# A two-layer hybrid block: each stream of the recurrent part gets its own build-time priority

## The chip, the cores and the metric

The program runs on one core of one Trainium2 chip, in one launch. The metric is the device time in microseconds (us) of that launch. Before the change the median of three runs is 3154.19 us (3151.38 to 3157.79); one further execution was taken with the hardware profiler.

## The reference, cut to what matters

Two layers work on 256 latent and 256 context tokens of width 1024. Each layer is a gated feed-forward part, a mixer with three branches (banded attention, an RWKV-7 recurrence, an S5 recurrence) that a gated sum merges, and a second feed-forward part. The change lies in the recurrent part of the mixer, the RWKV-7 branch:

```python
def rwkv7_scan(state0, r, decay, k, v, kk, kka, reverse):
    def step(state, inp):
        r_t, w_t, k_t, v_t, kk_t, b_t = inp
        state = (state * w_t[:, :, None, :]
                 - jnp.einsum('bhvk,bhk->bhv', state, kk_t)[..., None] * b_t[:, :, None, :]
                 + v_t[..., None] * k_t[:, :, None, :])
        return state, jnp.einsum('bhvk,bhk->bhv', state, r_t)
...
    s_f, ocf = rwkv7_scan(zero, rc, dfc, kc, vc, kkc, bc, reverse=False)
    s_b, ocb = rwkv7_scan(zero, rc, dbc, kc, vc, kkc, bc, reverse=True)
    _, olf = rwkv7_scan(s_f, rl, dfl, kl, vl, kkl, bl, reverse=False)
    _, olb = rwkv7_scan(s_b, rl, dbl, kl, vl, kkl, bl, reverse=True)
```

Eight heads of 64 channels are scanned forwards and backwards, first over the context, then over the latent tokens. Everything is in float32.

## The kernel before, in words

The kernel does not step token by token. It takes the heads in four pairs (p = 0 to 3) and the tokens in chunks of 64. For each pair, class Rwkv writes its work as generators:

- `operands()`: first `common()` (the low-rank inputs shared by all pairs), then `prep(p)`: it fetches or makes the pair's columns (`mixed`, `column`: a product with `w_in` whose weights go through `split`, lines 131 to 138), makes decay, normalised key and the chunk operands AR and BK. It stands still at marked places (`yield`), among them once after each of the two scan directions (d = 0, d = 1; lines 614 to 642).
- `fronts()`: `front(p)`: Gram products of the chunks (line 680, masked by L683), then the inverse of small triangular systems, the "solve": DMAs that gather 16x16 blocks, a chain of VectorE products and sums that each need the one before (L708, L709), DMAs that bring the result back (L727, L735).
- `turns()`: transposed operands. `backs()`: the rest of the inverse by TensorE products (L794) and VectorE (L803 to L819).
- `chains()`: the recurrence itself, eight chunk steps per pair, each TensorE, ScalarE (Y, L850), TensorE, both (Z, L863, L865), TensorE, VectorE (S, L878, L882).
- `ends()`: `finish(p)`: group norm, bonus and gate.

`conduct` (line 979) writes these generators into one program: it keeps a clock of its own that the generators' yields advance, always continues the first stream in its list that is due, and where none is due it continues a filler: dense products that have nothing to do with the recurrence (the gates and the remaining columns first, then the projections of the other branches). Layer 1 has all 15 of its recurrent columns made ahead and stored, layer 0 only 6; the other 9 are made inside `operands()`.

Two things set the order on the engines. TensorE's instructions stay in the order in which `conduct` wrote them (`manual_schedule` for PE). For VectorE (DVE), ScalarE (ACT), GpSimd (POOL) and the DMA queue of SyncE (SP), a planner orders the instructions when the program is built: it steps through a planned time, and an engine that is free takes, among the instructions whose inputs are ready in that plan, the one with the best priority. The priority is the place in the written program; `high_priority(offset=n)` counts an instruction as written n places earlier. Each engine then runs its list in that fixed order on the chip, whatever the real times. Before the change every one of the six streams has the same offset, HIGH = 300, and the filler has none:

```python
        with nullcontext() if s is filler else k.tc.high_priority(offset=HIGH):
            v = next(s.g, StopIteration)
```

The weights of the filler and of `column` pass through `split`: a DMA on SP (wr, L135), a rounded copy on ACT (wh, L136) and the remainder on DVE or, every second time in this part, on POOL (wl, L137); `mm3` multiplies with them in three products (L153 and L154 with wh, L155 with wl). Three buffers each hold wr, wh and wl, and two more each in layer 1's recurrent part.

Of the kernel before, what the change touches and what calls it, by code (L numbers as in the profile page):

```python
# [25 lines left out]
HIGH = 300  # L26
# [6 lines left out]
class Ctx:  # L33
    def __init__(self, ctx, tc):
        self.tc, self.nc = tc, tc.nc
        nc = self.nc
        self.cp = ctx.enter_context(tc.tile_pool(name="consts", bufs=1))
        self.wp = self.pool(ctx, "w")
        self.up = ctx.enter_context(tc.tile_pool(name="u", bufs=16))
        self.tp = ctx.enter_context(tc.tile_pool(name="tiny", bufs=2))  # L40
        self.dp = ctx.enter_context(tc.tile_pool(name="dram", bufs=1, space=DRAM))
        self.uid = 0
        self.aside = False
        self.mm = None
# [454 lines left out]
class Rwkv:  # L499
# [431 lines left out]
    def streams(self):  # L931

        pr = [{} for _ in range(4)]

        def chains():
            for p in range(4):
                yield f"prep{p}"
                yield from self.chain(pr[p])

        def turns():  # L940
            for p in range(4):
                yield f"prep{p}"
                for st in range(2):
                    yield from self.turn(pr[p], st)

        def backs():
            for p in range(4):
                yield f"front{p}"
                for st in range(2):
                    yield from self.back(pr[p], st)  # L950

        def ends():
            for p in range(4):
                yield f"chain{p}.1"
                yield from self.finish(pr[p])

        def operands():
            yield from self.common()
            for p in range(4):
                yield from self.prep(p, pr[p])  # L960

        def fronts():
            for p in range(4):
                yield f"prep{p}"
                yield from self.front(pr[p])

        return [Stream(g) for g in (fronts(), chains(), turns(), backs(), operands(), ends())]


class Stream:  # L970
# [1 line left out]

    def __init__(self, g):
        self.g, self.at, self.need = g, 0.0, None


def conduct(k, done, streams, filler, now, until):


    filler, dve = Stream(filler), now
    filler.at = now
    todo = streams + [filler]
    while filler in todo or until not in done:
        ready = [s for s in todo if s.need is None or s.need in done]
        s = next((s for s in ready if s.at <= now), None)
        if s is None:
            now = min(s.at for s in ready)
            continue  # L990
        with nullcontext() if s is filler else k.tc.high_priority(offset=HIGH):
            v = next(s.g, StopIteration)
        s.need = None
        if v is StopIteration:
            todo.remove(s)
        elif isinstance(v, str):
            s.need = v
        else:
            v = v if isinstance(v, tuple) else (1.0 if v is None else v, 0.3, None)
            now += v[0]  # L1000
            if len(v) == 3:
                dve = max(dve, now) + v[1]
            s.at = now if v[-1] is None else (now if len(v) == 2 else dve) + v[-1]
    return now, [s for s in todo if s is not filler]
# [596 lines left out]
def mixer(k, first, l, a, u, src, mods, mrows, acst, tab, ctx_out, spill):  # L1601
# [49 lines left out]
    with ExitStack() as es:  # L1651
        k.more_weights(es, f"mix{l}", None)
        with ExitStack() as e2:
            k.sp, k.qp = k.pool(e2, f"s5{l}"), k.pool(e2, f"att{l}")
            k.more_weights(e2, f"mixa{l}", (4, 4, 4))
            columns()
            k.sums.close()
            k.psum(e2, f"mixa{l}", 2, 2)
            rw = Rwkv(k, l, a, u, w_in, pf, ctx_out)
            dense = seq(rw.columns(), gates())  # L1660
            weave(k, local(), dense, W0[l], False)
            while rw.left:
                next(dense)
        k.more_weights(None, None, None)
        with ExitStack() as e2:
            e2.enter_context(tc.manual_schedule(engines={mybir.EngineType.PE}))
            k.psum(e2, f"mixr{l}", 2)
            k.sp, k.ep = k.pool(e2, f"rwl{l}"), k.pool(e2, f"rwe{l}")
            k.aside = True
            if not ctx_out:  # L1670
                k.more_weights(e2, f"mixr{l}", (2, 2, 2))
            streams = rw.streams()
            with ExitStack() as e3:
                k.qp = k.pool(e3, f"prep{l}")
                now, streams = conduct(k, rw.done, streams, dense, 0.0, "prep3")
            with ExitStack() as e3:
                k.qp = k.pool(e3, f"proj{l}")
                conduct(k, rw.done, streams, project(), now, "finish3")
            k.aside = False
# [179 lines left out]
```

## Time and profile before

| | before |
|---|---|
| median of 3 runs | 3154.19 us |
| profiled execution, its own time | 3158.24 us |
| its span, first to last instruction | 3156.4 us |
| mean granted TensorE clock | 0.931 |
| TensorE busy | 2774.0 us (88%) |
| VectorE, ScalarE, GpSimd busy | 1598.4, 1075.0, 747.4 us |

Instructions of the recurrent parts run from about 792 to 1270 us (layer 0) and from about 2490 to 2892 us (layer 1). Engines are named PE (TensorE), PEld (its weight loads), DVE, ACT, POOL and SP. "L803" is line 803 of the kernel; `X<-pt` says which tile is written from which.

### The profile page before, as it was taken

How to read it: one execution, taken by the hardware profiler on the slowest of the kernel's cores; microseconds unless marked ns; L12 is line 12 of the kernel's file. 1: busy time of each engine (PE TensorE's matmuls, PEld its weight loads, DVE VectorE, ACT ScalarE, POOL GpSimd, SP SyncE). 2: the span in 40 equal slices, each digit the busy share in tenths (PEclk: the TensorE clock that was granted, in tenths of full speed). 3: DMA queues.
4: the chain of work that ended last, by engine and by line, in shares of the span. 5: the costliest groups of instructions: out<-in, count | busy, mean ns of one | idle time of the engine just before them, and what ended most of it. 6: DMA issues, size and time to landing. Idle time of an engine off the chain costs nothing. (4 is left out here: it accounts for less than half of the span.)

```text
span 3156.4 us, 52345 instructions
## 1 busy us (share of the span) xinstructions
PE 2774.0 (88%) x19886; PEld 2184.1 (69%) x19886; DVE 1598.4 (51%) x3363; ACT 1075.0 (34%) x2132; POOL 747.4 (24%) x940
## 2 busy tenths in 40 slices
PE   4999999899887789889999989999988876688798
PEld 2666787658665566666678876778766775577697
DVE  4655235394355554542322577623559156654555
ACT  3222224244343322242232343322433352323453
POOL 1333004010232213430100335311311242113311
PEclk8999999999998889899999999999999797788899
DMA  7786544924442343568843354453482544154564
GB/s 225 210 245 200 155 142 138 236 66 121 117 109 48 71 97 96 185 196 269 269 122 94 110 137 126 119 158 121 120 216 75 140 129 109 34 122 139 167 186 152
DMA packets 656824, 455.22 MB, mean 144 GB/s; under 512 B 158982, under 2 KB 580980, under 8 KB 648380
## 3 DMA queue, kind: packets, MB, share of 16 engines
q1 hardware_dynamic: 604096, 415.30, 46.2%
q10 hardware_dynamic: 52476, 36.58, 4.2%
q8 instruction: 156, 2.56, 0.3%
q14 instruction: 96, 0.79, 0.1%
HBM read 391.26 MB, written 64.18 MB: 144 GB/s over the span
## 5 line engine op out<-in xcount | busy, mean ns | idle before, releaser
L153 PE MATMUL acc<-u,wh 128*128 128x512 f32 (+1 forms) x2544 | 935.2, 368 | 72.2 <-ACT wh L136 31.8
L155 PE MATMUL acc<-u,wl 128*128 128x512 f32 (+1 forms) x2544 | 917.6, 361 | 48.7 <-DVE wl L137 34.4
L154 PE MATMUL acc<-u,wh 128*128 128x512 f32 (+1 forms) x2544 | 917.1, 361 | 13.1 <-POOL u L289 9.9
L137 DVE TENSOR_TENSOR wl<-wr,wh 128x512 fp32r<-128x512 f32 x720 | 536.6, 754 | 758.1 <-ACT wh L136 746.1
L136 ACT CAST wh<-wr 128x512 fp32r<-128x512 f32 x844 | 513.2, 619 | 1055.9 <-PE acc L154 540.9
L153 PEld LDWEIGHTS acc<-u,wh 128*128 128x128 f32 x2544 | 499.5, 196 | 183.0 <-ACT wh L136 41.9
L155 PEld LDWEIGHTS acc<-u,wl 128*128 128x128 f32 x2544 | 499.7, 196 | 136.4 <-DVE wl L137 42.2
L154 PEld LDWEIGHTS acc<-u,wh 128*128 128x128 f32 x2544 | 500.4, 197 | 90.2 <-POOL u L289 17.9
L137 POOL TENSOR_TENSOR wl<-wr,wh 128x512 fp32r<-128x512 f32 x124 | 171.9, 1392 | 590.7 <-ACT wh L136 565.8
L365 POOL TENSOR_TENSOR hl<-sg,hh 128x512 fp32r<-128x512 f32 (+1 forms) x88 | 107.7, 1224 | 639.4 <-ACT hh L364 597.9
L398 PE MATMUL acc<-wl,hh 128*128 128x512 f32 x616 | 242.1, 393 | 0.0
L399 PE MATMUL acc<-wh,hl 128*128 128x512 f32 x616 | 242.1, 394 | 0.0
L397 PE MATMUL acc<-wh,hh 128*128 128x512 f32 x616 | 242.0, 393 | 0.0
L362 DVE TENSOR_TENSOR sg<-sg,acc 128x512 f32<-128x512 f32 (+1 forms) x88 | 54.6, 620 | 185.0 <-PE acc L155 184.8
L211 PE MATMUL pt<-wa,cond 128*32 128x512 f32 x576 | 101.5, 669 | 40.4 <-DMA wa<-in_w_ada_dram 40.4
L398 PEld LDWEIGHTS acc<-wl,hh 128*128 128x128 f32 x616 | 115.6, 188 | 25.7
L397 PEld LDWEIGHTS acc<-wh,hh 128*128 128x128 f32 x616 | 115.7, 188 | 25.5
L399 PEld LDWEIGHTS acc<-wh,hl 128*128 128x128 f32 x616 | 115.6, 188 | 25.4
L289 POOL TENSOR_TENSOR u<-v,u 128x256 fp32r<-128x256 f32 x88 | 71.4, 828 | 89.0 <-DVE v L288 86.6
L364 ACT CAST hh<-sg 128x512 fp32r<-128x512 f32 (+1 forms) x88 | 49.8, 566 | 105.0 <-DVE sg L362 104.8
L794 PE MATMUL pt<-X,X 64*64 64x64 f32 x1536 | 60.6, 242 | 26.6 <-DVE X L803 22.1
L794 PEld LDWEIGHTS pt<-X,X 64*64 64x64 f32 x1536 | 56.5, 156 | 32.2 <-issue 23.8
(345 smaller groups left out, 3633.2 us busy)
## 6 DMA issues: line engine op xcount, KB each, us to landing
wr<-in_ffn_w_in_dram SPq DMA_DIRECT2D x372, 256.0 KB
wa<-in_w_ada_dram SPq DMA_DIRECT2D x64, 1024.0 KB
wr<-in_w_in_dram SPq DMA_DIRECT2D x216, 256.0 KB
wr<-in_ffn_w_out_dram SPq DMA_DIRECT2D x176, 256.0 KB
s5r<-s5tab SPq DMA_DIRECT2D x24, 512.0 KB
wr<-in_branch_proj_dram SPq DMA_DIRECT2D x48, 256.0 KB
s5tab<-s5wo SPq DMA_DIRECT2D x64, 128.0 KB
s5tab<-s5wi SPq DMA_DIRECT2D x64, 128.0 KB
```

What stands on the lines that cost most here:

```text
L136: nc.scalar.copy(hi, raw)
L137: (nc.gpsimd if aside else nc.vector).tensor_tensor(lo, raw, hi.bitcast(F32), ALU.subtract)
L153: nc.tensor.matmul(ps, wh, xh, start=first, stop=False)
L154: nc.tensor.matmul(ps, wh, xl, start=False, stop=False)
L155: i = nc.tensor.matmul(ps, wl, xh, start=False, stop=last)
L211: nc.tensor.matmul(ps[32 * ci:32 * ci + 32, :], cond[:, kk, :], w[:, 512 * ci:512 * ci + 512], start=(kk == 0), stop=(kk == 7))
L289: nc.gpsimd.tensor_tensor(lo, v, hi.bitcast(F32), ALU.subtract)
L365: nc.gpsimd.tensor_tensor(h_lo[:, :ntok], sg[:, :ntok], h_hi.bitcast(F32)[:, :ntok], ALU.subtract)
L397: nc.tensor.matmul(ps, hh[f][:, tk], ws[0], start=n == 1, stop=False)
L398: nc.tensor.matmul(ps, hh[f][:, tk], ws[1], start=False, stop=False)
L399: nc.tensor.matmul(ps, hl[f][:, tk], ws[0], start=False, stop=n == nf)
L794: nc.tensor.matmul(ps[rows, j * C:(j + 1) * C], lhs(j, h, rows), rhs[rows, j * C:(j + 1) * C], start=True, stop=True)
```

## The change

Each stream carries its own offset in place of the common 300: fronts and chains 900, backs 600, turns and ends 300, operands 0. An offset of 0 is that of the filler. The program text that `conduct` writes, and with it the order on TensorE, depends on the yields alone and stays; no instruction is added or removed by the edit.

```diff
-        return [Stream(g) for g in (fronts(), chains(), turns(), backs(), operands(), ends())]
+        return [Stream(g, HIGH * x) for g, x in ((fronts(), 3), (chains(), 3), (turns(), 1), (backs(), 2), (operands(), 0), (ends(), 1))]
...
-    def __init__(self, g):
-        self.g, self.at, self.need = g, 0.0, None
+    def __init__(self, g, ahead=0):
+        self.g, self.ahead, self.at, self.need = g, ahead, 0.0, None
...
-        with nullcontext() if s is filler else k.tc.high_priority(offset=HIGH):
+        with k.tc.high_priority(offset=s.ahead) if s.ahead else nullcontext():
             v = next(s.g, StopIteration)
```

## Rows read from the trace of the kernel before

**Rows 1.** Stretches: length, busy us (instructions) of each engine, PE clock, DMA share.
```profile
945.00:1120.00 175.00, 132.62 (x1938) 106.97 (x1934) 101.26 (x208) 54.55 (x132) 39.02 (x48) 0.85 0.27 60
...
2490.00:2640.00 150.00, 102.93 (x847) 95.12 (x847) 71.27 (x104) 69.51 (x131) 54.14 (x49) 0.85 0.57 149
2640.00:2760.00 120.00, 84.52 (x1572) 72.62 (x1570) 75.38 (x173) 39.82 (x104) 20.52 (x24) 0.78 0.22 45
```

**Rows 2.** TensorE's waits, 792 to 1270 us: us in total, times, longest.
```profile
PE pt L794 <- DVE X L803: 19.7, 3, 9.2
PE pt L857 <- ACT Y L850: 18.6, 11, 6.5
PE acc L155 <- DVE wl L137: 11.0, 2, 9.3
...
PE acc L155 <- POOL wl L137: 4.8, 2, 4.0
```

**Rows 3.** TensorE's waits, 910 to 927 us.
```profile
PE acc L153 <- ACT wh L136: 3.5, 1, 3.5
```

**Rows 4.** TensorE's waits, 2490 to 2892 us.
```profile
PE pt L794 <- DMA X<-sysr: 18.8, 3, 15.8
PE acc L155 <- DVE wl L137: 17.0, 3, 12.3
PE pt L857 <- ACT Y L850: 14.4, 15, 5.5
PE acc L153 <- ACT wh L136: 14.0, 2, 12.6
```

**Rows 5.** Timeline of DVE from 830 us: start, us, engine, line, operation, tiles, count.
```profile
830.41 1.39 DVE L635 TENSOR_TENSOR AR<-dc,kk 128x252 f32<-128x252 f32 x1
...
834.03 0.42 DVE L642 TENSOR_TENSOR BK<-dc,z 64x256 f32<-64x256 f32 x1
834.48 1.29 DVE L137 TENSOR_TENSOR wl<-wr,wh 128x512 fp32r<-128x512 f32 x2
```

**Rows 6.** Timeline of ACT from 911 us.
```profile
911.08 0.29 ACT L634 COPY AR<-kk 128x4 f32<-128x4 f32 x2
...
913.71 1.66 ACT L136 CAST wh<-wr 128x512 fp32r<-128x512 f32 x3
```

**Rows 7.** Timeline of POOL from 914 us.
```profile
914.98 2.94 POOL L642 TENSOR_TENSOR BK<-dc,z 64x256 f32<-64x256 f32 x4
917.88 3.12 POOL L137 TENSOR_TENSOR wl<-wr,wh 128x512 fp32r<-128x512 f32 x2
```

**Rows 8.** Timeline of SP, DMA issues from 2496 us.
```profile
2496.08 0.43 SPq L565 DMA_DIRECT2D lw<-in_rwkv_w_dram  x1
...
2498.68 0.98 SPq L135 DMA_DIRECT2D wr<-in_w_in_dram  x2
```

**Rows 9.** Timeline of DVE from 2608 us.
```profile
2608.01 0.94 DVE L635 TENSOR_TENSOR AR<-dc,kk 128x252 f32<-128x252 f32 x1
2608.88 0.67 DVE L709 TENSOR_REDUCE sysT<-X 128x64 f32<-128x512 f32 x1
...
2614.81 0.42 DVE L642 TENSOR_TENSOR BK<-dc,z 64x256 f32<-64x256 f32 x1
2615.26 1.89 DVE L137 TENSOR_TENSOR wl<-wr,wh 128x512 fp32r<-128x512 f32 x3
```

**Rows 10.** Timeline of ACT from 990 us.
```profile
990.03 1.28 ACT L615 ACT_TABLE_LOAD   x1
...
996.32 0.25 ACT L850 COPY Y<-pt 128x128 f32<-128x128 f32 x1
```

**Rows 11.** Line 635 from 785 to 1130 us: duration ns min/median/max.
```profile
L635 DVE TENSOR_TENSOR AR<-dc,kk x16: 414/422/1401, 821.3 to 1100.3; 128x252 f32<-128x252 f32 x16
```

**Rows 12.** Timeline of TensorE: the Gram products of pair 2, layer 0.
```profile
1035.40 0.83 PE L680 MATMUL pt<-AR,BK 64*128 64x128 f32 x10
```

**Rows 13.** Timeline of DVE: the last operands of pair 2, layer 0.
```profile
1022.51 0.76 DVE L642 TENSOR_TENSOR BK<-dc,z 64x256 f32<-64x256 f32 x2
```

**Rows 14.** Groups on DVE by form, 2713 to 2719 us: busy us, mean ns.
```profile
L683 DVE TENSOR_TENSOR G<-pt,cst 128x512 f32<-128x512 f32 x4 | 2.5, 681 | 0.0
L683 DVE TENSOR_TENSOR G<-pt,cst 128x256 f32<-128x256 f32 x4 | 1.5, 418 | 0.1
```

## The prediction

> **What bounds the kernel now.** I read the stretches first. TensorE is the busiest engine, but not in the recurrent parts: from 945 to 1120 us it works 132.6 of 175 us, and 102.9 of 150 and 84.5 of 120 us in two stretches of layer 1, at a granted clock of 0.85, 0.85 and 0.78 of full speed, means of time at its two levels of 1.2 and 2.4 GHz [rows 1]. There it is held by others, so the second view is the list of its waits. They fall into two kinds. The first are waits of the recurrence itself: 19.7 us on X of `back`, 18.6 on Y of `chain` in layer 0 [rows 2], 14.4 on Y and 18.8 on the solve's DMA in layer 1 [rows 4]. The second are waits of dense products on a split of their weights: 11.0 on VectorE and 4.8 on GpSimd in layer 0 [rows 2], 3.5 on ScalarE [rows 3], 17.0 on VectorE and 14.0 on ScalarE in layer 1 [rows 4]. The third view, the timeline of the engine that ended each long wait, shows the same in nearly all: a run of `prep` instructions of the next pair just ahead of the one that TensorE needs.
>
> **What the change can move.** It changes offsets, so it moves an instruction only where two are ready together in the plan and the new difference of offsets turns their order. Two cases have to be kept apart.
>
> Streams against each other (900, 600, 300 in place of 300 for all): the written order already decided between them, and `conduct` writes in TensorE's order. The second half of a pair's operands is written behind the normalisation's products (L190), and the chain's step of that moment stands ahead of these. So Y of 996.32 us had the better place already, and still ran behind 6.3 us of `prep` on ScalarE (from 990.03, where a table load of 1.28 us begins) [rows 10]: the plan did not have it ready when the chip did. A higher offset does not cure that. The recurrence's waits could fall by anything from nothing to all 52.7 us of the three largest VectorE and ScalarE rows (19.7 + 18.6 + 14.4); I take 3 us, near the lower end, for the few short operations (a finish, an early `prep` part) that were written earlier and ready.
>
> Operands against the filler (0 against 0, before 300 against 0): here the order does turn. Until now every `prep` instruction went ahead of a filler split written up to 300 places earlier. Now the written order decides, and since `conduct` gives the filler its turn between the two directions of the operands (the yield between them states 4.6 us of VectorE time), a column begun there has its splits ahead of the second direction.
>
> - Layer 0, wait of 9.3 us [rows 2]: the split at 834.48 had eight `prep` instructions of the second direction ahead of it, from 830.41 on [rows 5]. It gains 834.48 - 830.41 = 4.1; the first direction stays ahead. Bounds 0 and 9.3.
> - Layer 0, 910 to 927 us: 3.5 on ScalarE [rows 3], 4.0 on GpSimd and 11.0 - 9.3 = 1.7 on VectorE [rows 2]. ScalarE's cast at 913.71 stood behind `prep` from 911.08: 2.6. GpSimd's split stood behind four L642, 2.9 [rows 6, 7]. With the 1.7 that is 7.2; bounds 0 and 9.2.
> - Layer 1, 12.6 us at its start [rows 4]: on SP the weight load at 2498.68 was issued behind the operand loads that begin at 2496.08 [rows 8]; `common` stays ahead, the pair's loads go behind: 2.6. Bounds 0 and 12.6, because the weights' landing is most of it.
> - Layer 1, the other two VectorE waits: 17.0 - 12.3 = 4.7; I take 4.0, the size of the second direction in layer 0. Bounds 0 and 4.7.
> - Layer 1, 12.3 us [rows 4]: the split at 2615.26 had `prep` ahead from 2608.01, with one solve reduction of 0.67 that stays ahead [rows 9]: 7.25 - 0.67 = 6.6. Bounds 0 and 12.3.
>
> Together 3 + 4.1 + 7.2 + 2.6 + 4.0 + 6.6 = 27.5 us.
>
> **What it gives back.** The moved splits now run beside GpSimd's half of the operands. L635 takes 414 ns alone and up to 1401 ns in these runs [rows 11]; I charge the difference, 1.0 us, at five places: 5 us; bounds 0 and 7. The operands come later by the splits put ahead of them (0.7 us each); their reader, the Gram products, had room where I looked: the last operand of pair 2 began at 1022.51 and the products at 1035.40, 12.1 us after its end [rows 12, 13]. So no charge there; without that room each 0.7 would show. Last, part of each removed wait comes back at the next one: three weight buffers let a split run only a column or so ahead, and TensorE arrives sooner at the next. I take a third, 9.2 us, between nothing and all of it. The nine columns that layer 0 makes inside `operands()` lose their 300 places too; they then come in TensorE's own order with the filler's, which is worth nothing either way in the sum. The sum is 27.5 - 5 - 9.2 = 13.3 us.
>
> The Trainium skill has a rule that speaks against this part ("SBUF — State Buffer", Who interferes with whom): a VectorE instruction with two SBUF inputs and a GpSimd instruction that reads SBUF exclude each other, and whichever is issued second waits the other out in full. The spread of L635 agrees [rows 11]. By it a moved split could wait out a whole GpSimd operand, and the GpSimd one a moved split: my estimate from the page's rule is twice the 5 us, and the sum would be 8.3 us instead of 13.3.
>
> **From the profiled execution to the median.** The rows come from an execution of 3158.2 us (span 3156.4, 1.8 around it). 3158.2 - 13.3 = 3144.9. That execution was 4.0 us above the median of 3154.2, so the median to expect is 3141.
>
> **The rivals.**
>
> 1. *The recurrence gains too.* If the planner did hold the chain's and the solve's instructions back in favour of the operands, X, Y and the solve win: half of 19.7 + 18.6 + 14.4 and half of the longest solve wait of 15.8, 34 us more: 3107. For it: the runs of `prep` stand right ahead of these too [rows 10]. Against it: equal offsets and the written order already favoured them.
> 2. *Next to nothing changes.* The splits were not ready in the plan either when the operands began, or the next wait takes all of the gain. Then within 6 us of before: 3153. For it: the Y case shows that plan and chip differ by microseconds. Against it: TensorE waited at L155, with the first two products of the same weights behind it, so the cast that the split needs had long been done.
> 3. *Slower: the operands starve.* With the lowest rank, each handoff of a pair's normalisation (square, root, spread, two products that TensorE waits for) can find a mask block of `front` ahead on VectorE: eight L683 are 2.5 + 1.5 = 4.0 us [rows 14]. Three pairs per layer run beside another pair, each with two handoffs: 12 x 4.0 = 48 us at most. It decides from 27.5 - 14.2 = 13.3 us, some four of the twelve; with six of them, 24 us, the result is 3154.2 - 13.3 + 24 = 3165. For it: TensorE's order is fixed, so a late product stops all behind it. Against it: the Gram products of the pair before stand ahead of these handoffs in TensorE's order, so their masks are mostly done by then.
>
> **How the numbers follow.** About 0.2%, 6.3 us, is what a measurement can tell from no change. Chances: the forecast 0.50 (own range 3126 to 3150), rival 1 0.12, rival 2 0.20, rival 3 0.18. Faster: 0.12 and nearly all of 0.50, 0.60 in all; same 0.22 (rival 2 and the upper edge of the forecast); slower 0.18. The range reaches down to half of rival 1's extra gain, which leaves 0.08 below, and up to 3161, which takes in rival 2 and the first part of rival 3 and leaves about 0.12 above: 3118 to 3161. The five splits' upper bounds (9.3 + 9.2 + 12.6 + 4.7 + 12.3 = 48.1) lie below its lower end and count to the part left out; all lower bounds with the charge of 7 fall at 3161.
>
> **What the changed profile would show.** TensorE's waits on wl L137 by VectorE fall from 11.0 to about 7 in layer 0 and from 17.0 to about 6 in layer 1; that on GpSimd's from 4.8 to about 1; the 12.6 at layer 1's start to about 10, with the weight load ahead of z and v on SP. X on L803 and Y on L850 stay above 30 us in layer 0. If those two fall by half, my reading of the plan is wrong (rival 1). New waits of L181, L190, L654 or L680 on `prep`, beyond 13 us in sum, make it slower (rival 3).

## The result and the profile after

The changed kernel takes 3112.1 us (median of 4 runs, 3106.08 to 3115.16), the kernel before beside it 3155.99 us (4 runs, 3151.38 to 3164.49): a ratio of 0.9858, 95% interval 0.9842 to 0.9875. It is faster by some 44 us, where 13 were forecast, and 6 us below the lower end of the range. The number came out close to rival 1 (3107), and rival 1's mechanism is the one that the runs below show; that its sum fits so well is in part luck, as the part on the rivals says.

The profiled run took 3109.57 us. The page of the kernel after, its span and the busy time of each engine:

```profile
span 3107.8 us, 52359 instructions
PE 2772.4 (89%) x19886; PEld 2180.3 (70%) x19886; DVE 1595.0 (51%) x3363; ACT 1082.4 (35%) x2140; POOL 746.0 (24%) x940
```

TensorE does the same work in the same order, and no engine became busier by more than the 7.4 us of ScalarE (eight more instructions, all of them table loads: 47 in place of 39). So the 48.6 us between the two spans (3156.4 - 3107.8) lie in waits and in the clock, not in work. The order on TensorE being the same, the same matmul can be looked up in both traces: from one matmul ahead of the recurrent part to one behind it, layer 0 went from 489.3 to 457.9 us and layer 1 from 423.4 to 408.6, so 31.4 + 14.8 = 46.2 us lie there.

The stretches of the kernel after that hold the work of [rows 1] (start and end moved by the shift of the matmuls at their edges; columns as there):

```profile
935.00:1090.00 155.00, 135.88 (x1950) 108.66 (x1946) 96.95 (x206) 52.98 (x131) 39.05 (x48) 0.87 0.28 61
2455.00:2599.00 144.00, 105.70 (x897) 98.09 (x898) 74.11 (x105) 76.36 (x137) 52.32 (x50) 0.88 0.58 152
2599.00:2711.00 112.00, 83.31 (x1524) 70.09 (x1520) 73.92 (x172) 40.60 (x105) 22.01 (x26) 0.79 0.26 51
```

The first stretch is 20 us shorter with TensorE's work nearly the same, the other two are 14 us shorter together (their common edge lies some 50 matmuls further on than before, so they are not compared one by one); the granted clock is nearly what it was.

TensorE's waits in the kernel after, layer 0 (794 to 1241 us, which answers to [rows 2, 3]):

```profile
PE acc L155 <- DVE wl L137: 9.5, 2, 7.7
PE pt L190 <- ACT X L186: 6.5, 3, 4.1
PE pt L857 <- ACT Y L850: 5.0, 10, 0.7
...
PE pt L794 <- DVE X L803: 3.1, 1, 3.1
...
PE pt L181 <- ACT o L918: 2.8, 1, 2.8
PE pt L857 <- DVE G L683: 2.7, 1, 2.7
...
PE acc L155 <- POOL wl L137: 0.9, 1, 0.9
```

And layer 1 (2455 to 2845 us, which answers to [rows 4]; lines behind the constructor of the streams are one higher after the change):

```profile
PE acc L153 <- ACT st L1631: 17.8, 8, 5.3
PE pt L794 <- DMA X<-sysr: 17.6, 5, 6.9
PE pt L857 <- ACT Y L850: 10.9, 14, 3.1
PE acc L153 <- ACT wh L136: 9.7, 1, 9.7
...
PE acc L155 <- DVE wl L137: 3.4, 3, 1.8
```

The solve's wait in layer 1 hardly fell (18.8 to 17.6 us). Most of it stands at two neighbouring groups of matmuls, 6.9 and 6.6 us, where it was 15.8 and 1.9 before. In s600_o300 (below) the whole wait is 7.6. SP at that place, in the kernel after and then in s600_o300:

```profile
2708.56 0.91 SPq L1406 DMA_DIRECT2D gw<-in_s_glu_w_dram  x2
2709.63 6.57 SPq L735 DMA_DIRECT2D X<-sysr  x4
```

```profile
2738.61 0.48 SPq L1406 DMA_DIRECT2D gw<-in_s_glu_w_dram  x1
2739.32 2.55 SPq L735 DMA_DIRECT2D X<-sysr  x4
```

In the kernel after the four transfers that bring X are issued over 6.57 us, behind two loads of weights for the projections (gw), in s600_o300 over 2.55 us, behind one. Whether those loads are the reason was not tested.

The waits of the recurrence that fell most are those of which I had said that they would stay: X from 19.7 to 3.1 and Y from 18.6 to 5.0 in layer 0. How that looks on the engine, in the kernel after, on ScalarE (start, us, line, operation):

```profile
981.75 1.28 ACT L615 ACT_TABLE_LOAD   x1
983.05 0.63 ACT L615 ACTIVATE dc<-dc 128x512 f32<-128x512 f32 x1
983.58 0.25 ACT L850 COPY Y<-pt 128x128 f32<-128x128 f32 x1
983.85 1.28 ACT L585 ACT_TABLE_LOAD   x1
```

It is the place of [rows 10]. There Y began 6.3 us after the first table load of `prep`, behind all of the run. Here it stands after the first instruction of that run, 1.8 us after the table load, and the rest of `prep` follows it.

### The profile page after: what moved, and what is told of

The parts are those of the page before. It is cut to its first block, busy times and chain, and to the rows that moved or that the text cites. A ratio compares the mean times of both kernels' runs of the same rounds, so it can differ in the third digit from the quotient of the medians.

```text
span 3107.8 us, 52359 instructions
## 1 busy us (share of the span) xinstructions
PE 2772.4 (89%) x19886; PEld 2180.3 (70%) x19886; DVE 1595.0 (51%) x3363; ACT 1082.4 (35%) x2140; POOL 746.0 (24%) x940
## 5 line engine op out<-in xcount | busy, mean ns | idle before, releaser
L155 PE MATMUL acc<-u,wl 128*128 128x512 f32 (+1 forms) x2544 | 916.2, 360 | 27.5 <-DVE wl L137 19.0
L154 PE MATMUL acc<-u,wh 128*128 128x512 f32 (+1 forms) x2544 | 915.6, 360 | 17.4 <-POOL u L289 11.1
L155 PEld LDWEIGHTS acc<-u,wl 128*128 128x128 f32 x2544 | 498.9, 196 | 113.7 <-DVE wl L137 27.7
L269 ACT ACTIVATE nrm<-x,nb,rstd 128x512 f32<-128x512 f32 x44 | 33.9, 808 | 123.5 <-DVE nb L266 109.5
L211 PEld LDWEIGHTS pt<-wa,cond 128*32 128x32 f32 x576 | 16.2, 112 | 83.5 <-issue 47.3
```

What stands on the lines that cost most here:

```text
L154: nc.tensor.matmul(ps, wh, xl, start=False, stop=False)
L155: i = nc.tensor.matmul(ps, wl, xh, start=False, stop=last)
L211: nc.tensor.matmul(ps[32 * ci:32 * ci + 32, :], cond[:, kk, :], w[:, 512 * ci:512 * ci + 512], start=(kk == 0), stop=(kk == 7))
```

## The experiments

The theory that all runs test, called A: the builder's counter of places goes back when a step under an offset ends, so that only the filler (and a stream without an offset) moves it on. With equal offsets a place therefore counts from the beginning of the instruction's own step, not of the program. The `prep` instructions of a pair's second half stand in short steps (18 instructions for one scan direction in layer 0) and beat Y and X, which stand behind the matmuls of their own step (8 calls ahead of Y, 4 in a pair's first step, and 16 ahead of X; each call is two instructions in the trace). By this theory the written order, on which the prediction rested, did not decide between the streams. The builder's own code is not shown here; the theory is inferred from the runs, above all from flat0 against flat300, which have all streams and the filler at one rank and differ, inside the recurrent parts, in the counter alone. The rivals stand in the expectations.

Six groups of TensorE's waits, in us, from the list of waits of each kernel (780 to 1290 us, and 2440 to 2910 us). "Offsets" are those of fronts, chains, turns, backs, operands, ends in units of 300; the filler has 0 where nothing is said.

| kernel | offsets | ratio to before | layer 0: X L803 | Y | VectorE wl | layer 1: X<-sysr | Y | VectorE wl at L155 |
|---|---|---|---|---|---|---|---|---|
| before | all 1 | 1 | 19.7 | 18.6 | 11.0 | 18.8 | 14.4 | 17.0 |
| after | 3 3 1 2 0 1 | 0.9858 | 3.1 | 5.0 | 9.5 | 17.6 | 10.9 | 3.4 |
| e1_operands_0 | 1 1 1 1 0 1 | 0.9874 | 3.1 | 7.0 | 9.5 | 20.3 | 11.5 | 2.9 |
| s600_o300 | 2 2 2 2 1 2 | 0.9929 | 3.2 | 11.0 | 11.1 | 7.6 | 10.6 | 16.4 |
| o240 | 1 1 1 1 0.8 1 | 0.9972 | 3.2 | 11.6 | 11.1 | 8.3 | 10.9 | 20.7 |
| written300 | all 1, counter moved on | 0.9966 | 4.8 | 8.7 | 10.1 | 7.1 | 10.1 | 20.7 |
| flat0 | all 0 | 0.9890 | 4.8 | 8.0 | 9.6 | 7.1 | 8.8 | 3.2 |
| flat300 | all 1, filler 1 | 1.0034 | 26.7 | 17.9 | 1.3 | 45.6 | 13.9 | 0 |
| written_ranks | as after, counter moved on | 0.9826 | 3.1 | 7.3 | 9.5 | 11.1 | 12.0 | 3.3 |
| ops_m100 | 3 3 1 2 -1/3 1 | 0.9800 | 3.2 | 11.3 | 1.4 | 8.9 | 11.5 | 0.5 |
| ops_m300 | 3 3 1 2 -1 1 | 0.9824 | 4.0 | 8.9 | 1.4 | 10.0 | 10.6 | 1.1 |

**e1_operands_0: the operands lose their offset, all other streams keep 300.**

```diff
-... ((fronts(), 3), (chains(), 3), (turns(), 1), (backs(), 2), (operands(), 0), (ends(), 1))]
+... ((fronts(), 1), (chains(), 1), (turns(), 1), (backs(), 1), (operands(), 0), (ends(), 1))]
```

> Operands at offset 0, all five other streams back at 300: the one demotion of the change without its ranks. Theory A (a stream's place is counted within its step, because the counter of places goes back when a step with an offset ends; so a short prep step beats everything that stands behind a row of matmuls in its own step, and taking the operands' offset away ends that): nearly the whole gain, ratio to before 0.983 to 0.989, X on L803 in layer 0 under 5 us, Y on L850 under 8 us. Rival C (the ranks of solve and chains over the other streams bring the gain): at most half of it, ratio 0.992 or more. Rival B (the prediction's reading: written order already decided, only the tie with the filler counts): ratio 0.993 or more with X and Y above 30 us.

Measured: 3119.32 us (4 runs), 0.9874 (0.9846 to 0.9901), against 0.9858 for the full change, the intervals overlapping. The operands' 0 alone brings nearly all of the gain, the recurrence's part included. This kernel was ahead of the full change for a while. At the same matmul (1144 us in the kernel before) it was 35.7 us ahead of the kernel before, the full change 29.3; a little later (1160 us), where the filler has become the projections of the other branches, 16.8 and 23.1. One wait is most of these 18.9 us, and the order on SP has part in it. The list of TensorE's waits of e1_operands_0, its timeline of SP, and a line of SP in the kernel after:

```profile
PE acc L153 <- ACT u L1016: 19.6, 3, 12.1
```

```profile
1116.63 0.36 SPq L1395 DMA_DIRECT2D yu<-s5y  x1
1117.22 4.22 SPq L727 DMA_DIRECT2D sysr<-sysT  x8
1121.55 1.39 SPq L1570 DMA_DIRECT2D yu<-atty  x3
```

```profile
1113.53 6.65 SPq L1570 DMA_DIRECT2D yu<-atty  x2
```

The load that u needs (L1570) is issued at 1121.55, behind eight transfers of the solve (4.22 us) and behind the loads of L1394 and L1395; in the kernel after it is issued at 1113.53, and the solve's transfers come later. So whether ranks above 300 for the chain and the solve bring anything of their own is not told apart by this pair.

**s600_o300: the operands stay 300 above the filler, the others go 300 above them.**

```diff
+... ((fronts(), 2), (chains(), 2), (turns(), 2), (backs(), 2), (operands(), 1), (ends(), 2))]
```

> Operands keep 300 over the filler, the five other streams go to 600: operands behind the other streams, but still ahead of the filler. Theory A: the recurrence's waits go (X and Y in layer 0 from 38 us together to under 15), the dense products' waits on wl behind prep stay (9.3 and 12.3 us within 3 us); gain 20 to 35 us, ratio 0.989 to 0.994. Rival B: nothing moves in the recurrence, ratio 0.998 to 1.002. Rival C gives no different number from B here, since the five streams stay equal among themselves.

Measured: 3138.20 us (5 runs), 0.9929 (0.9906 to 0.9952). Putting the recurrence ahead of the operands is worth 0.0071 x 3157.7 = 22 us by itself in this run; o240, below, has nearly the same waits and gains 9. The waits of its layer 0:

```profile
PE acc L155 <- DVE wl L137: 11.1, 2, 9.3
PE pt L857 <- ACT Y L850: 11.0, 11, 4.9
...
PE acc L155 <- POOL wl L137: 4.8, 2, 4.1
```

The splits' waits are those of [rows 2] (11.0 and 4.8), Y fell from 18.6 to 11.0 and X from 19.7 to 3.2. The two effects can be separated, and the recurrence's is there without the splits'.

**written300: equal offsets as before, but the counter moves on by what a step wrote.** This is the program that the prediction thought it was reading.

```diff
         with k.tc.high_priority(offset=s.ahead) if s.ahead else nullcontext():
+            at = k.tc.cur_priority
             v = next(s.g, StopIteration)
+            wrote = k.tc.cur_priority - at
+        if s.ahead:
+            k.tc.cur_priority += wrote
```

The list of streams has 1 for all six.

> All six streams at 300 as before, but the counter of places is moved on by what each step wrote, so that places are those of the written program. Theory A: X and Y in layer 0 fall from 38 us to under 20 although no stream is ranked over another; ratio 0.988 to 0.996. Rival B, by which this is the order that was in force already: ratio 0.998 to 1.002 and X and Y unchanged. Rival C: no gain without ranks, ratio 0.998 or more.

Measured: 3146.51 us (10 runs), 0.9966 (0.9946 to 0.9987). With no stream ranked above another, X falls from 19.7 to 4.8 and Y from 18.6 to 8.7 in layer 0, and the solve's wait from 18.8 to 7.1 in layer 1. When the written order does decide, most of these waits are not there. In the kernel before, then, it did not. The ratio lies just above theory A's range (0.988 to 0.996): of the 40.8 us by which X, Y and the solve's wait fall (Y in both layers), only 0.0034 x 3157.7 = 11 us reach the time. TensorE waits longer elsewhere, on u (22.6 in both layers, 11.1 before), on wh in layer 1 (18.3, 14.0 before) and on VectorE's wl there (20.7, 17.0 before). A wait that goes is not a time that is gained.

**o240: all at 300, the operands 60 places lower.**

```diff
+... [Stream(g, int(HIGH * x)) for g, x in ((fronts(), 1), ..., (operands(), 0.8), (ends(), 1))]
```

> As before, five streams at 300, but operands at 240: sixty places lower, and still 240 ahead of the filler. Theory A (places count from each step's beginning, and no step of prep's second half writes much over 30 instructions): sixty places are as good as three hundred; X in layer 0 falls from 22.6 to 4 to 8 us, Y from 18.6 to under 13, the wl waits stay at 9 to 12 (layer 0) and 14 to 20 us (layer 1); ratio 0.990 to 0.996. If written places counted from the beginning of the program, sixty of them would turn few orders: X and Y above 30 us together, ratio 0.998 to 1.002.

Measured: 3145.69 us (10 runs), 0.9972 (0.9954 to 0.9989). Sixty places do to X and Y what three hundred do (3.2 and 11.6 against 3.2 and 11.0 in s600_o300). So the places that were compared in the kernel before lay within a few tens of each other, as places counted from the beginning of a step do. The ratio misses theory A's range here, too (0.990 to 0.996; X was to be 4 to 8 us, VectorE's wl in layer 1 at most 20). The orders of o240 and s600_o300 differ at few places (33 of 3363 on VectorE, 29 of 2093 on ScalarE without its table loads, 15 of 1615 on SP), and their profiled executions took 3140.69 and 3138.60 us, yet their ratios, taken beside different runs of the kernel before, are 0.0043 apart, some 14 us. So what the recurrence is worth alone is known as 9 to 22 us, no closer.

**flat0: no stream has an offset.** Every instruction then moves the counter on.

```diff
+... ((fronts(), 0), (chains(), 0), (turns(), 0), (backs(), 0), (operands(), 0), (ends(), 0))]
```

> No offset for any stream: streams, operands and filler all in the written order. Theory A: X, Y and the wl waits behind prep all shrink, but Z, S and Y now stand behind filler splits and sigmoids of 0.6 to 1.9 us that were written earlier; ratio 0.985 to 0.995, Z and S waits up by 2 to 6 us. Rival B: only the wl waits shrink, ratio 0.994 to 0.999 with X and Y above 30 us. Rival C: no gain without ranks, ratio 0.998 or more.

Measured: 3124.11 us (4 runs), 0.9890 (0.9867 to 0.9914). Nothing is ranked above anything, and 0.0110 x 3157.7 = 35 us are gained: most of what the change brings comes without any rank, by the end of a preference that no offset stated. Of the price that was expected (Z and S up by 2 to 6 us) S in layer 1 shows 3.9 us (7.5 to 11.4); in layer 0 neither rose.

**flat300: filler and streams all at 300, so that no step moves the counter on.** All are equal, as in flat0, and inside the recurrent parts only the counter differs.

```diff
+... ((fronts(), 1), (chains(), 1), (turns(), 1), (backs(), 1), (operands(), 1), (ends(), 1))]
...
-    filler, dve = Stream(filler), now
+    filler, dve = Stream(filler, HIGH), now
```

> The filler at 300 too, all else as before: operands tie with the filler, and also still with the other streams; no step moves the counter on, so every place counts within its step. Theory A: a filler split stands at the beginning of its step, so the wl waits behind prep shrink (28.0 us over both layers to under 18), while Y in layer 0 keeps its 18.6 us within 4 us and X stays above 15; ratio 0.988 to 0.996. By the prediction's reading the same first half and an equal recurrence, so this one separates the two halves of the gain, not A from B: the tie with the filler alone is worth the measured difference, 10 us by the prediction's net terms, 17 us by the difference of the runs with operands at 0 and at 300 under streams of 300 and 600.

Measured: 3168.28 us (10 runs), 1.0034 (1.0018 to 1.0050): slower than before, outside the expected range (0.988 to 0.996), and 1.4 points slower than flat0. That X and Y stay (26.7 and 17.9) and the splits' waits go was expected; that the whole gets slower was not. In layer 1, with TensorE's longest wait on the solve, and the timeline of SP in that wait:

```profile
PE pt L794 <- DMA X<-sysr: 45.6, 6, 27.9
```

```profile
2757.39 0.59 SPq L1394 DMA_DIRECT2D yu<-s5u  x1
2758.08 1.67 SPq L727 DMA_DIRECT2D sysr<-sysT  x2
2761.51 0.38 SPq L1395 DMA_DIRECT2D yu<-s5y  x1
2763.11 0.38 SPq L1394 DMA_DIRECT2D yu<-s5u  x1
2763.54 1.10 SPq L727 DMA_DIRECT2D sysr<-sysT  x2
...
2774.96 2.55 SPq L735 DMA_DIRECT2D X<-sysr  x4
```

The loads of yu (L1394, L1395) belong to the filler's projections; by theory A their places, too, count from the beginning of their own step here, and are no longer behind the solve's. They stand between the solve's transfers on SP, and the eight L727 that carry the solve's result out are spread from 2758 to 2772 us (in e1_operands_0 eight of them took 4.22 us in one piece). X, which TensorE waits for, is issued behind the last, at 2774.96. This is the rival on the other side that the prediction did not have: not operands that starve, but a solve that does.

**ops0_backs3 and after_again: how far the same order scatters.** The first ranks backs 900; all engines and SP then have the instruction order of the kernel after, so it is a repeat, as the second is.

```diff
+... ((fronts(), 3), (chains(), 3), (turns(), 1), (backs(), 3), (operands(), 0), (ends(), 1))]
```

> The change with backs at 900 like fronts and chains (operands 0, turns and ends 300). Theory A: operands' rank is all that matters, ratio within 0.004 of the change's own in this job. Rival C (ranks of solve and chains): backs now tie with them, so part of the ranks' gain would go, 0.003 to 0.008 above the change's.

> The changed kernel unchanged, in the same job, to hold the others against: ratio 0.984 to 0.988.

Measured: 3106.87 us, 0.9868 (0.9836 to 0.9900), and 3104.04 us, 0.9850 (0.9829 to 0.9871), 4 runs each. Three measurements of one order (the two and the change's own 0.9858) lie within 0.0018; with the order unchanged, the rank of backs is without effect.

**gates_300: the sigmoid of the gates (st) gets 300, too.** It aims at the new largest wait of layer 1, 17.8 us.

```diff
+            with tc.high_priority(offset=HIGH):
                 nc.scalar.activation(t[:, :tok], ps[:, :tok], AF.Sigmoid)
```

> The change, and the sigmoid that empties the gates' sums (L1631) at 300 instead of 0, so that it goes ahead of prep's work on ScalarE. In the changed kernel TensorE waits 17.8 us on it in layer 1 (12.5 before). If those waits are a matter of rank, 6 to 12 us of them go and the time falls 5 to 10 us below the change's; if it is the table loads of 1.28 us between exponential and sigmoid, the time stays within 4 us of it.

Measured: 3106.85 us (4 runs), 0.9859 (0.9836 to 0.9882): no gain. The waits on st fall from 17.8 (19.9 in the repeat) to 13.7, those of the splits rise from 3.4 to 7.1 and of tm from 4.0 to 6.2. Some 4 us went of the 6 to 12 that a rank was to take, and they came back elsewhere: the wait is traded, not removed. Whether the table loads keep it up is not shown.

**written_ranks: the ranks of the change with the counter moved on, as in written300.**

> The change with the counter moved on by every step, so that places are those of the written program under the ranks 900, 900, 300, 600, 0, 300. Theory A: with operands at the bottom rank it hardly matters how places are counted, ratio within 0.004 of the change's 0.985 to 0.986. If the counting mattered in its own right (not only through operands against the rest), it would move by more.

Measured: 3106.12 us (4 runs), 0.9826 (0.9808 to 0.9844); in layer 1 the solve's wait is 11.1 in place of 17.6. A little better than the change, but the interval overlaps that of the repeat (0.9829 to 0.9871).

**ops_m100 and ops_m300: the operands behind the filler, too.**

```diff
+... [Stream(g, int(HIGH * x)) for g, x in (..., (backs(), 2), (operands(), -1/3), (ends(), 1))]
```

> The change with operands at -100, a hundred places behind the filler. Theory A: whatever prep still puts ahead of filler splits goes too (a wait of 7.7 us on wl in layer 0), but operands now wait for casts and sigmoids of the filler, so waits of L181 and L190 on prep rise by 3 to 10 us; ratio 0.982 to 0.990. If the operands are already late enough at 0, the second effect wins: 0.988 to 0.995.

> The kernel after with the operands 300 places behind the filler (-300) in place of 0; with -100 the ratio to before was 0.9800, with 0 it was 0.985 to 0.987. Theory A (a place inside the own step, so lower only matters until every split and chain step of the moment is ahead of the operands): -100 has emptied the VectorE wl waits already (1.4 and 0.0 us), so -300 finds none left; what it can still move are the operands' own consumers, and the ratio stays within 0.004 of 0.9800. Rival (the operands starve, rival 3 of the prediction): with -300 the operands come behind the next columns' splits too, waits of L680 and L654 and of the column's normalisation grow by more than 12 us, ratio 0.985 or more.

Measured: 3096.44 us (4 runs), 0.9800 (0.9778 to 0.9822) for -100, the best of all and clear of the intervals of the change and of its repeat; 3105.66 us (5 runs), 0.9824 (0.9800 to 0.9847) for -300. For -100 that is better than theory A's range (0.982 to 0.990). The change itself was not run beside ops_m100; written_ranks was, and its interval overlaps, so the size of the further gain is open. The list of waits of ops_m100, layer 0, around the splits, and a line of layer 1:

```profile
PE pt L181 <- ACT tm L590: 4.8, 3, 2.3
...
PE acc L155 <- DVE wl L137: 1.4, 1, 1.4
```

```profile
PE pt L181 <- ACT tm L590: 9.2, 2, 4.9
```

VectorE's split wait of 9.5 that the change leaves in layer 0 is 1.4, and 3.4 in layer 1 is 0.5. The price is in the operands' own chain (tm 0.6 to 4.8 in layer 0, 4.0 to 9.2 in layer 1). At -300 no further gain shows, and the operands do not starve there either (1.0 us of waiting at L680). The diff is that of ops_m100; ops_m300 has -1 in place of -1/3.

## Why the prediction was wrong, step by step

**The step that failed** is "the written order already decided between them", from which "a higher offset does not cure that" and 3 us for the whole recurrence followed. By the rows, the recurrence's waits fell by 16.6 (X) + 13.6 (Y) in layer 0 and 3.5 (Y) + 1.2 (X<-sysr) in layer 1, 34.9 us in place of 3. The explanation that "the plan did not have it ready when the chip did" was argued from one timeline and is refuted for most of these waits by written300 and o240: X and part of Y come in time as soon as their places are the program's or 60 places better. For the 8.7 and 11.6 us of Y that these two leave in layer 0 it may still hold. Rival 1, which had the mechanism, got 0.12; what should have been asked is how a place is counted when a step is written under an offset. The prediction's own tell worked: X and Y were to stay above 30 us, and fell to 8.1. One bound was also not what its words say: half of rival 1's extra 34 us below 3141 is 3124, not 3118; the measured time lies below both.

**The splits**, predicted and measured:

| term | predicted gain | measured | from |
|---|---|---|---|
| wait of 9.3, layer 0 | 4.1 | 7.5 | 9.3 to 1.8 (9.5 - 7.7) |
| 910 to 927 us, layer 0 | 7.2 | 1.5 | 3.5 + 4.0 + 1.7 to one wait of 7.7 |
| 12.6 at layer 1's start | 2.6 | 2.9 | 12.6 to 9.7 |
| other waits on VectorE's wl, layer 1 | 4.0 + 6.6 | 13.6 | 17.0 to 3.4 |

Their sum, 25.5, is near the 24.5 predicted, with the shares wrong. The first gap in the timeline of VectorE, kernel after (it answers to [rows 5]):

```profile
834.60 0.42 DVE L642 TENSOR_TENSOR BK<-dc,z 64x256 f32<-64x256 f32 x1
835.05 0.69 DVE L137 TENSOR_TENSOR wl<-wr,wh 128x512 fp32r<-128x512 f32 x1
835.65 0.41 DVE L635 TENSOR_TENSOR AR<-dc,kk 128x252 f32<-128x252 f32 x1
```

The split stands ahead of the second direction and behind the first, as forecast. In the second stretch, though, "the first direction stays ahead" is what kept the wait:

```profile
907.99 1.80 DVE L601 SCALAR_TENSOR_TENSOR tm<-z,pf,z 128x512 f32<-128x512 f32 x1
...
913.27 0.42 DVE L642 TENSOR_TENSOR BK<-dc,z 64x256 f32<-64x256 f32 x1
913.72 0.69 DVE L137 TENSOR_TENSOR wl<-wr,wh 128x512 fp32r<-128x512 f32 x1
```

The casts and GpSimd's splits came earlier as predicted (3.5 to 0, 4.8 to 0.9), and TensorE then waited 7.7 us at the next split, which had the first direction ahead of it. The clause "part of each removed wait comes back at the next one" fits here, but at 7.7 of 9.2, not at a third. ops_m100, which puts the split ahead of most of that direction as well (it begins at 906.38 there, behind L601 and one L641), empties it.

At layer 1's start the order on SP is the one that was read from the diff: the weight load ahead of the pair's operands (SP of the kernel after, answering to [rows 8]).

```profile
2461.02 0.98 SPq L135 DMA_DIRECT2D wr<-in_w_in_dram  x2
2462.04 0.50 SPq L565 DMA_DIRECT2D lw<-in_rwkv_w_dram  x1
...
2463.14 1.06 SPq L539 DMA_DIRECT2D z<-rwz  x2
```

**What it gives back.** Charged were 5 us for VectorE beside GpSimd and 9.2 for next waits. The slowing is there: line 635, 785 to 1100 us, kernel after, against [rows 11]:

```profile
L635 DVE TENSOR_TENSOR AR<-dc,kk x16: 410/422/2343, 824.3 to 1082.4; 128x252 f32<-128x252 f32 x16
```

Its longest went from 1401 to 2343 ns, with the median at 422 ns in both. But VectorE's whole busy time fell from 1598.4 to 1595.0 us and GpSimd's from 747.4 to 746.0, so no 5 us show in them. The rule of the Trainium skill ("SBUF — State Buffer", Who interferes with whom), that a VectorE instruction with two SBUF inputs contends with a GpSimd instruction that reads SBUF, agrees with that spread (L635 has two such inputs, and GpSimd worked on its half of the operands beside the longest one); the doubled charge worked out from it does not show in these sums. Waits that are new or longer, besides the 7.7: st 12.5 to 17.8 in layer 1, G 2.7 once in each layer, o 2.8, X of L186 4.1 to 6.5 in layer 0. That is 5.3 + 5.4 + 2.8 + 2.4 = 15.9 us, a little more than the 14.2 charged; gates_300 shows that a rank takes only part of the largest, and without a gain. Two of them in the kernel before, layer 0 and layer 1:

```profile
PE pt L190 <- ACT X L186: 4.1, 1, 4.1
```

```profile
PE acc L153 <- ACT st L1630: 12.5, 8, 5.0
```

**Summed up:** the rows of the recurrence gain 34.9, those of the splits 25.5 and 15.9 are given back: 44.5 remain, against the 46.2 us between the same matmuls. All waits of TensorE in the two recurrent parts (792 to 1273 and 2490 to 2895 us in the kernel before, the same matmuls in the kernel after), rows left out above included, fell from 87.3 to 55.0 and from 111.5 to 96.3 us, 47.5 in all; its busy time there rose by 1.3. How much of it belongs to which rank is not a sum: the recurrence ahead of the operands is worth 9 to 22 us alone (o240, written300, s600_o300), and the operands level with the filler brings another 17 to 31 on top (e1_operands_0 against these three). The prediction had 3 us for the first and 24.5 - 14.2 = 10.3 for the second, so the second was too small as well, though its mechanism is there. Against s600_o300, e1_operands_0 waits 30.3 us less on splits and casts in the two parts, and 12.7 us more on the solve in layer 1; flat300, with every stream level with the filler, gains nothing: the solve's wait is 26.8 us longer there than in the kernel before.

**The rivals.** Rival 1's mechanism is what happened: streams that stood behind the operands gain. Its sum fits in part by luck: it had 26.4 us from X and Y and 7.9 from the solve, measured are 33.7 and 1.2. Rival 2 is excluded by the interval. Rival 3, operands that starve, would show at L181 and L190: 4.8 us before, 9.9 after in layer 0, 7.5 and 6.2 in layer 1, no wait at L680 or L654; 3.8 us more in all, under the 13.3 from which it decides. Whether ranks of 900 and 600 add anything to 300 stays open: e1_operands_0 and the change differ by less than their intervals.

## What to carry to other kernels

Before arguing from priorities, find out how a place is counted: with equal offsets, a counter that goes back after each step compares places within steps, so what stands near the beginning of a short step wins. What can be late without anyone waiting (operands of the next pair) belongs behind everything else, the filler's splits included; one list entry did that, and going further (-100) gave the best time here. Waits that go are not all gained: price a change by the time of runs that differ in it alone. A rank orders the DMA queue as well: look at who stands between two transfers of a serial chain there.

## What the runs showed of the hardware that was not expected

One stretch outside the recurrent part has the same 110 or so matmuls, back to back, in all kernels, and ran at either of two speeds: from its first matmul to its 113th it took 13.1 to 13.4 us in nine of the fourteen profiled executions and 18.7 to 19.9 in five. The stretch from its first matmul on, in the kernel before (20 us), in the kernel after (13 us) and in ops0_backs3 (20 us), columns as in [rows 1]:

```profile
2458.00:2478.00 20.00, 20.00 (x114) 19.71 (x114) 1.44 (x2) 2.19 (x4) 1.33 (x3) 0.63 0.61 156
```

```profile
2430.00:2443.00 13.00, 13.00 (x112) 12.86 (x112) 2.26 (x2) 2.02 (x4) 1.33 (x3) 0.99 0.91 236
```

```profile
2432.00:2452.00 20.00, 20.00 (x114) 19.71 (x114) 1.44 (x2) 2.27 (x4) 1.33 (x3) 0.63 0.58 150
```

At 0.99 TensorE runs at 2.4 GHz nearly all the time, at 0.63 for much of it at 1.2 GHz, and that is worth 6.8 us (12.8 against 19.6 between the same two matmuls). ops0_backs3 has the order of the kernel after on every engine and still got the lower value, so this part of the profiled difference (some 7 of 48.6 us) is not set by the order of the instructions; it makes single profiled runs differ, and the ratios of several runs are the better measure. What TensorE did ahead of the stretch was nearly the same, 12.24 of 14 us busy in the kernel before and 13.07 of 15 in the kernel after, at a granted 0.82 and 0.80; what decides between the two levels stays open.
